# Empty rows of blocks are not gathered, places are permuted evenly, and the last 12 blocks add into sums in SBUF

## The chip, the cores and the metric

The kernel runs on one core of a Trainium2 chip. The metric is the device time of one execution in microseconds. TensorE (PE) multiplies, VectorE (DVE), ScalarE (ACT) and GpSimd (POOL) do the elementwise work, and 16 DMA engines, shared by all queues, move data between DRAM and SBUF. Two queues matter here: the one that SyncE (SP) feeds carries the weights, and the one that POOL feeds carries the gathers and scatters of rows.

## The reference, cut to what matters

One post-norm layer on x (512 tokens of 1024): a mixer of sparse and differential attention, attention into 256 memory tokens, then a mixture of experts; each is followed by a LayerNorm of `ALPHA * h + sublayer(h)`. The change concerns the experts alone:

```
scores = sigmoid(xf @ router_w)                      # 512 x 64
top_e  = top_k(scores + router_bias, 8)              # 8 experts of 64 for a token
gates  = scores[top_e] / sum(scores[top_e]) * 2.5
for e in experts:
    rows = tokens that chose e
    acc[rows] += swiglu(xf[rows], w_gate[e], w_up[e], w_down[e]) * gates
h = layer_norm(ALPHA * xf + acc + shared_swiglu(xf))
```

Each expert has 3.146 MB of fp32 weights (gate and up 1024 x 256 each, down 256 x 1024). 512 tokens of 8 experts make 4096 rows in all.

## The kernel before, in words

The attention parts run first (to about 580 us). Then the router ranks the experts by their number of rows, and they are done in 66 blocks: four fixed experts, 60 by rank, and two blocks with the overflow of the two largest. A rank has a fixed capacity from the list `CAPS` (128 down to 48 places; two of 160), 5392 places in all, so 1296 are empty. Counted from the reference's own inputs, the empty places are 296 in the first four blocks, 379 in blocks 4 to 23, 417 in blocks 24 to 53 (179 of them in 40 to 53) and 204 in the last twelve blocks, which have 656 places.

`meta` lists the rows of up to four ranks at a time: `one_hot` compares the places with each token's position, four small matmuls turn that into numbers, and `finish_meta` makes from them a gather index (`gidx`: an empty place reads row 0), a scatter index (`sidx`: an empty place goes to a spare row behind the 512 real ones) and the gate (`gsl`). `gather` (L1220) fetches the rows of a block by an indirect DMA into a tile `xg` (three buffers), `AHEAD` = 2 blocks ahead. A block of more than 64 rows is wide: its weights are split into two parts (`split_w`) and multiplied in three matmuls. From about block 38 on blocks are narrow (`narrow_block`): TensorE transposes `xg` into `xn` (L1268, L1271), multiplies with gate and up in plain fp32 (L1280), ACT makes `sg` (L1299), DVE `hm` (L1304), which is transposed into `ht` (L1313, L1315) and multiplied with `wd` (L1291) one block later, and ACT copies the output into `y` (L1294).

`scatter` (L1332) adds `y` to the rows of `acc`, a tensor in DRAM that holds the residual and the shared expert, by an indirect DMA with accumulation. All scatters write the same tensor, so each waits until the one before has landed. POOL issues gathers and scatters in the order of its program. SP issues the weight loads (L1226, L1235), `LEAD` = 9 loads of 1 MB ahead of the block that uses them, when one of the 18 free buffers of the pool `slots` is there; weights, their split parts and `y` (one buffer for two blocks) share that pool. After the last scatter (L1332, last of 66) `acc` is read back into `h` by four loads (L1625), and the last LayerNorm (L171, L1639) writes the output.

Of the kernel before, what the change touches and what calls it, by code (L numbers as in the profile page):

```python
# [19 lines left out]
P = 128  # L20
# [20 lines left out]
BIG_AT = (30, 50)  # L41
# [5 lines left out]
CAPS = ([128] * FIX + [160, 160, 128, 128] + [112] * 4 + [96] * 14 + [80] * 12 + [64] * 19 + [48] * 7)  # L47
HALF = 64
# [10 lines left out]
def encoder_layer(  # L59
# [927 lines left out]
    slot_id = cst.tile([P, P + 32], F32, name="slot_id")  # L987
# [4 lines left out]
    def dispatch_consts():  # L992
        jp = wk([P, P], name="jp")
        nc.gpsimd.iota(jp, pattern=[[1, P]], base=0, channel_multiplier=-1, allow_small_or_imprecise_dtypes=True)
        nc.vector.tensor_scalar(tri, jp, 0.0, None, op0=OP.is_gt)
        nc.vector.memset(ones, 1.0)
        nc.gpsimd.iota(slot_id, pattern=[[1, P + 32]], base=0, channel_multiplier=0,
                       allow_small_or_imprecise_dtypes=True)
# [42 lines left out]

    posf = cst.tile([P, NT, FIX], F32, name="posf")
# [132 lines left out]
    gidx = cst.tile([P, NEXP + 2], I32, name="gidx")  # L1175
# [12 lines left out]
    def one_hot(poscol, first=0, w=P):  # L1188
        oh = wk([P, NT, P], F32R, name="oh")[:, :, 0:w]
        nc.vector.tensor_tensor(oh, slot_id[:, None, first:first + w].to_broadcast([P, NT, w]),  # L1190
                                poscol.to_broadcast([P, NT, w]), op=OP.is_equal)
        return oh
# [7 lines left out]
    def meta(cols):  # L1200
# [4 lines left out]
        po, va = (posf, valf) if cols[-1][1] < FIX else (pos, vals)  # L1205
        for e, (c, r, first) in enumerate(cols):
            ohs.append(one_hot(po[:, :, r:r + 1], first, w))
# [6 lines left out]
        finish_meta(ps[0:w, 0:n * 4].rearrange("p (e v) -> p e v", v=4), n, gidx[0:w, s], sidx[0:w, s], gsl[0:w, s], w)  # L1214
# [68 lines left out]
    def narrow_out(m, ht, wd, n):  # L1283

        if m % 2 == 0:
            Y["y"] = slot([P, 2, D], name="y")
        y = Y["y"][:, m % 2, :]
        ps = bank()
        for j in range(2):
            for c in range(2):  # L1290
                nc.tensor.matmul(ps[HALF * c:HALF * c + n, :], lhsT=ht[:, j, 0:n], rhs=wd[:, j, c * 512:(c + 1) * 512],  # L1291
                                 start=j == 0, stop=j == 1)
        for c in range(2):
            nc.scalar.copy(y[0:n, c * 512:(c + 1) * 512], ps[HALF * c:HALF * c + n, :])  # L1294
        return y

# [93 lines left out]
    metas = [[(r, r, 0) for r in range(a, min(a + GRP, NEXP))] for a in range(FIX + 2, NEXP, GRP)]  # L1390
# [4 lines left out]
    NB = len(blocks)  # L1395
    W, XG, GS = {}, {}, {}
# [18 lines left out]
    def fetch_x(m):  # L1415
        if m < NB:
            _, _, n, c = blocks[m]
            XG[m] = gather(gidx[:, c:c + 1], n)
# [62 lines left out]
    def finish(m, ht, n, wd, si):  # L1481
        if narrow(m):
            y = narrow_out(m, ht, wd, n)
# [3 lines left out]
        scatter(y, si, n)  # L1487
# [6 lines left out]
    def narrow_block(m, X, xt, gs, si):  # L1494
        r, _, n, _ = blocks[m]
        step = 3 * step_of[r]
        ps = bank()
        w = W[r]
        narrow_mm(xt, w, n, ps, range(KH))
        yield 0.45 * KH, 0.0  # L1500
        ht = expert_h(*BEFORE[0][0:2])
        narrow_mm(xt, w, n, ps, range(KH, KD))
        yield 0.9, 0.0
# [8 lines left out]
        yield 0.8, 0.0  # L1512
# [3 lines left out]
    def experts():  # L1516
# [48 lines left out]
        finish(NB - 1, expert_h(*BEFORE[0][0:2]), *BEFORE[0][1:])  # L1565

# [23 lines left out]
    with tc.For_i(0, left, 1) as k:  # L1590
# [15 lines left out]
        gi = small.tile([P, 1], I32, name="gi", bufs=2)  # L1606
        si = small.tile([P, 1], I32, name="si", bufs=2)
        gs = small.tile([P, 1], F32, name="gs", bufs=2)
        finish_meta(ps[:, 0:4].rearrange("p (e v) -> p e v", v=4), 1, gi, si, gs)
        xg = gather(gi)  # L1610
# [5 lines left out]
        ht = expert_h(expert_mid(expert_gate(pg), pu, gs))  # L1616
        for c in range(2):
            y = expert_out(0, ht, w3[2], c)
        scatter(y, si)
# [3 lines left out]
    h3 = [slot([P, 2, D], name="h") for _ in range(2)]  # L1623
    for t in range(NT):
        nc.sync.dma_start(h3[t // 2][:, t % 2, :], acc[t * P:(t + 1) * P, :])  # L1625
    st = []
    for t in range(NT):
        h = h3[t // 2][:, t % 2, :]
# [5 lines left out]
    for t in range(NT):  # L1634
        h = h3[t // 2][:, t % 2, :]
# [38 lines left out]
```

## Time and profile before

| | us |
|---|---|
| median of 3 runs | 1315.51 |
| lowest, highest | 1314.42, 1317.23 |
| profiled execution, its own time | 1310.08 |
| its span in the trace | 1308.3 |
| TensorE busy in the span | 1155.8 (88%) |
| VectorE, ScalarE, GpSimd busy | 748.5, 562.0, 439.5 |

The busy times are averages over stages with different limits: from 640 to 850 us the wide blocks, from 850 to 1187 us wide and then narrow ones, from 1187 to 1271 us the last blocks up to the last matmul, and after that the last scatters and the LayerNorm. The rows by stage are shown below. The profiled execution is 5.4 us under the median of the three timed runs.

### The profile page before, as it was taken

What the parts mean: (1) busy time and instruction counts of PE and PEld (TensorE: products, weight loads), DVE (VectorE), ACT (ScalarE), POOL (GpSimd) and SP (SyncE); (2) the same over time, 40 slices, a digit from 0 to 9 for tenths busy, and PEclk for the clock granted to TensorE, in tenths of its full rate; (3) what the DMA queues carried; (4) which work ended last, traced back from release to release, by engine and by line L of the source; (5) the groups of instructions that cost most, each with busy time, mean ns of one, the idle gap of its engine ahead of it and who ended that gap; (6) DMA issues with size and microseconds to landing.
All of it is one profiled execution on the core that took longest, in us unless ns stands there. A gap on an engine that the chain in (4) does not pass through costs nothing. (4 is left out here: it accounts for less than half of the span.)

```text
span 1308.3 us, 20859 instructions
## 1 busy us (share of the span) xinstructions
PE 1155.8 (88%) x7768; PEld 908.2 (69%) x7768; DVE 748.5 (57%) x1617; ACT 562.0 (43%) x1006; POOL 439.5 (34%) x288
## 2 busy tenths in 40 slices
PE   3999999999898899889999999999899988897770
PEld 2887778988898898878778777777667544553330
DVE  7168986566865557787767777666465211311114
ACT  3235456644454453335555556555454211321122
POOL 4333444542236343552212323232213222223213
PEclk9999999998999899999999999999999989998995
DMA  7322234463326256688999999999999999999974
GB/s 225 86 74 65 58 103 114 121 202 116 126 67 210 63 185 208 226 332 329 299 289 331 352 347 362 332 359 359 350 367 338 350 347 387 363 363 353 349 279 141
DMA packets 136807, 324.67 MB, mean 248 GB/s; under 512 B 12001, under 2 KB 94945, under 8 KB 111873
## 3 DMA queue, kind: packets, MB, share of 16 engines
q1 hardware_dynamic: 119984, 275.83, 58.2%
q0 software_dynamic: 13632, 46.80, 14.8%
q8 instruction: 62, 1.02, 0.3%
q10 hardware_dynamic: 3088, 0.69, 0.2%
q14 instruction: 41, 0.33, 0.1%
HBM read 288.10 MB, written 35.19 MB: 247 GB/s over the span
## 5 line engine op out<-in xcount | busy, mean ns | idle before, releaser
L95 POOL TENSOR_TENSOR whl<-wraw,whl 128x1024 fp32r<-128x1024 f32 x81 | 195.9, 2419 | 265.4 <-ACT whl L94 239.4
L1244 DVE TENSOR_TENSOR whl<-wraw,whl 128x1024 fp32r<-128x1024 f32 x152 | 182.9, 1231 | 85.7 <-ACT whl L1243 79.6
L1332 POOL DMA_INDIRECT acc<-y,sidx x66 | 104.8, 1587 | 361.5 <-DMA acc<-y,sidx 161.4
L101 PE MATMUL ps<-whl,xt 128*96 128x256 f32 (+4 forms) x640 | 184.3, 288 | 5.6 <-ACT whl L1243 3.9
L103 PE MATMUL ps<-whl,xt 128*96 128x256 f32 (+4 forms) x640 | 179.8, 281 | 1.9 <-DVE xt L95 1.9
L102 PE MATMUL ps<-whl,xt 128*96 128x256 f32 (+4 forms) x640 | 179.6, 281 | 0.6 <-DVE whl L1244 0.6
L1243 ACT CAST whl<-wraw 128x1024 fp32r<-128x1024 f32 x152 | 152.5, 1053 | 27.9 <-DMA wraw<-in_e_w_gate_dram 20.0
L1327 PE MATMUL ps<-wd,ht 128*96 128x512 f32 (+4 forms) x320 | 147.1, 603 | 4.0 <-DVE ht L1315 3.8
L1280 PE MATMUL ps<-wraw,xn 128*64 128x256 f32 (+1 forms) x832 | 116.8, 404 | 27.0 <-DMA wraw<-in_e_w_up_dram 12.2
L1220 POOL DMA_INDIRECT xg<-rows,gidx x66 | 76.5, 1159 | 160.3 <-PE ps L1252 62.5
L1299 ACT ACTIVATE sg<-ps 64x256 f32<-64x256 f32 (+6 forms) x66 | 25.0, 378 | 239.6 <-PE ps L1280 127.1
L94 ACT CAST whl<-wraw 128x1024 fp32r<-128x1024 f32 x91 | 95.4, 1048 | 57.1 <-PE ps L103 46.5
L101 PEld LDWEIGHTS ps<-whl,xt 128*96 128x96 f32 (+4 forms) x640 | 104.3, 163 | 6.8 <-ACT whl L1243 4.1
L103 PEld LDWEIGHTS ps<-whl,xt 128*96 128x96 f32 (+4 forms) x640 | 104.3, 163 | 2.9 <-DVE xt L95 2.6
L1280 PEld LDWEIGHTS ps<-wraw,xn 128*64 128x64 f32 (+1 forms) x832 | 60.6, 140 | 65.0 <-DMA wraw<-in_e_w_up_dram 15.8
L102 PEld LDWEIGHTS ps<-whl,xt 128*96 128x96 f32 (+4 forms) x640 | 104.5, 163 | 1.1 <-DVE whl L1244 0.7
L1327 PEld LDWEIGHTS ps<-wd,ht 128*96 128x96 f32 (+4 forms) x320 | 49.5, 164 | 72.9 <-issue 66.0
L1315 DVE COPY ht<-ps 128x128 f32<-128x128 f32 (+6 forms) x66 | 21.4, 324 | 96.3 <-PE ps L1313 96.3
L1328 ACT COPY y<-ps 96x512 f32<-96x512 f32 (+4 forms) x80 | 46.3, 582 | 68.8 <-PE ps L1327 67.4
L1304 DVE SCALAR_TENSOR_TENSOR hm<-ps,og,sg 64x256 f32<-64x256 f32 (+4 forms) x54 | 36.8, 681 | 58.0 <-ACT sg L1299 48.8
L101 PE MATMUL ps<-xTh,whl 128*128 128x512 f32 (+1 forms) x168 | 65.6, 390 | 0.0
L103 PE MATMUL ps<-xTh,whl 128*128 128x512 f32 (+1 forms) x168 | 63.8, 380 | 0.0
(421 smaller groups left out, 2756.7 us busy)
## 6 DMA issues: line engine op xcount, KB each, us to landing
wraw<-in_e_w_gate_dram SPq DMA_DIRECT2D x64, 1024.0 KB, 18.8
wraw<-in_e_w_up_dram SPq DMA_DIRECT2D x64, 1024.0 KB, 15.7
wd<-in_e_w_down_dram SPq DMA_DIRECT2D x64, 1024.0 KB, 18.0
wraw<-in_w_in_dram SPq DMA_DIRECT2D x21, 512.0 KB, 3.7
wraw<-in_m_wkv_dram SPq DMA_DIRECT2D x16, 512.0 KB, 4.2
wraw<-in_m_wq_dram SPq DMA_DIRECT2D x16, 512.0 KB, 3.9
wraw<-in_m_wo_dram SPq DMA_DIRECT2D x16, 512.0 KB, 3.9
wraw<-in_w_o_dram SPq DMA_DIRECT2D x12, 512.0 KB, 3.5
```

Of the source, the lines that this page charges most:

```text
L94: nc.scalar.copy(hi, src)
L95: eng.tensor_sub(lo, src, hi.bitcast(F32))
L101: nc.tensor.matmul(ps, lhsT=a, rhs=b, start=start, stop=False)
L102: nc.tensor.matmul(ps, lhsT=a, rhs=bl, start=False, stop=False)
L103: nc.tensor.matmul(ps, lhsT=al, rhs=b, start=False, stop=stop)
L1220: nc.gpsimd.indirect_dma_start(out=xg[0:n, :], out_offset=None, in_=rows, in_offset=bass.IndirectOffsetOnAxis(ap=gi[0:n, :], axis=0))
L1243: nc.scalar.copy(hi[v], w[i][v])
L1244: lo_eng.tensor_sub(lo[v], w[i][v], hi[v].bitcast(F32))
L1280: nc.tensor.matmul(ps[HALF * i:HALF * i + n, 0:256], lhsT=xt[:, k, 0:n], rhs=w[i][:, k, :], start=k == 0, stop=k == KD - 1)
L1327: nc.tensor.matmul(ps[0:n, :], lhsT=ht[:, j, 0:n], rhs=wd[:, j, cs], start=j == 0, stop=j == 1)
L1328: nc.scalar.copy(y[0:n, cs], ps[0:n, :])
L1332: nc.gpsimd.indirect_dma_start(out=acc, out_offset=bass.IndirectOffsetOnAxis(ap=si[0:n, :], axis=0), in_=y[0:n, :], in_offset=None, comput ...
```

## The change

1. `gather` takes `sidx`, with a bound of the last real row: an index beyond it, that of an empty place, is skipped and moves nothing. `gidx` goes. The scatters of the empty places into spare rows stay.
2. Places are numbered by tables (`place_of`, small POOL iotas) that spread a rank's real rows evenly over the block's partitions. `meta` therefore groups only ranks of equal capacity; the second of the two experts of 160 is done at block 48 and not at 50.
3. The last `SUMMED` = 12 blocks (54 to 65, all narrow) have no scatter. `summed_out` writes the output of a block as a pair of fp32r parts `yp`, two blocks of 64 partitions in one tile, and for each pair of blocks `add_sums` multiplies it with a one-hot matrix of the tokens: 8 steps of two 128 x 512 matmuls and a DVE add into `sums`, two tiles of `slots` with the whole `acc`. `start_sums` takes five buffers at block 55, `load_sums` loads `acc` into `sums` on POOL's queue at block 56, after the scatter of block 53. Steps are interleaved with the blocks (`flush`), four in a block; twelve stand behind the last block. The LayerNorm reads `sums`; the four loads of `h` go. The lead of the weights is 10 loads in the last blocks.

```
-    def finish_meta(pv, n, gi, si, gs, w=P):
-        nc.vector.tensor_copy(gi, pv[:, :, 0])
+    def finish_meta(pv, n, si, gs, w=P):
...
+    def place_of(n, first):
...
+                        nc.gpsimd.iota(v, pattern=[[1, b], [16, hi - lo]], base=first + g * b + 16 * ((lo - g) % m),
+                                       channel_multiplier=0, allow_small_or_imprecise_dtypes=True)
...
     def gather(gi, n=P):
         nc.gpsimd.indirect_dma_start(out=xg[0:n, :], out_offset=None, in_=rows,
-                                     in_offset=bass.IndirectOffsetOnAxis(ap=gi[0:n, :], axis=0))
+                                     in_offset=bass.IndirectOffsetOnAxis(ap=gi[0:n, :], axis=0),
+                                     bounds_check=SEQ - 1, oob_is_err=False)
...
+    def load_sums():
+        for u in range(2):
+            a = slot([P, 2, D], name="sums")
+            for t in range(2):
+                nc.gpsimd.dma_start(a[:, t, :], acc[(2 * u + t) * P:(2 * u + t + 1) * P, :])
+                ACC.append(a[:, t, :])
...
+    def add_sums(oh, yp):
+        for t in range(NT):
+            for c in range(2):
+                cs = slice(c * 512, (c + 1) * 512)
+                ps = bank()
+                for l in range(2):
+                    nc.tensor.matmul(ps, lhsT=oh[:, t * P:(t + 1) * P], rhs=yp[:, l, cs], start=l == 0, stop=l == 1)
+                nc.vector.tensor_add(ACC[t][:, cs], ACC[t][:, cs], ps)
+                yield
...
+    def summed_out(m, ht, wd, n, si):
...
+        for cs, v in halves:
+            nc.scalar.copy(yp[r, 0, cs], v)
+        for cs, v in halves:
+            nc.vector.tensor_sub(yp[r, 1, cs], v, yp[r, 0, cs].bitcast(F32))
+        if i % 2:
+            oh = OHS[1][p % 3]
+            one_hot_rows(oh, STF.pop(p))
+            READY.append(add_sums(oh, PAIR.pop(p)))
...
     def finish(m, ht, n, wd, si):
-        if narrow(m):
-            y = narrow_out(m, ht, wd, n)
+        if m >= M0:
+            summed_out(m, ht, wd, n, si)
+        elif narrow(m):
+            scatter(narrow_out(m, ht, wd, n), si, n)
...
+        if m == M0 + 1:
+            start_sums()
+        if m == M0 + 2:
+            load_sums()
...
         finish(NB - 1, expert_h(*BEFORE[0][0:2]), *BEFORE[0][1:])
+        FL.extend(READY)
+        flush(16)
...
-    h3 = [slot([P, 2, D], name="h") for _ in range(2)]
-    for t in range(NT):
-        nc.sync.dma_start(h3[t // 2][:, t % 2, :], acc[t * P:(t + 1) * P, :])
```

POOL's program around the end of the scatters, of before; `xg` are gathered rows, the line with `acc` is a scatter, and the second row is the scatter of block 53:

```order
L1220 DMA xg<-rows,gidx 64x1024
L1332 DMA acc<-y,sidx 640x1024
L1220 DMA xg<-rows,gidx 48x1024
L1332 DMA acc<-y,sidx 640x1024
L1220 DMA xg<-rows,gidx 48x1024
L1332 DMA acc<-y,sidx 640x1024
L1220 DMA xg<-rows,gidx 48x1024 x2
L1332 DMA acc<-y,sidx 640x1024 x2
```

The same place after; L1327 are the four loads of `sums`, and the scatter ahead of them is that of block 53:

```order
L1245 DMA xg<-rows,sidx 64x1024
L1430 DMA acc<-y,sidx 640x1024
L1320 IOTA tk 128x512
L1245 DMA xg<-rows,sidx 64x1024
L1430 DMA acc<-y,sidx 640x1024
L1245 DMA xg<-rows,sidx 48x1024 x2
L1327 DMA sums<-acc 128x1024 x4
L1245 DMA xg<-rows,sidx 48x1024 x2
```

The loads stand behind the gathers of blocks 59 and 60, ahead of those of blocks 61 and 62, and no scatter follows.

DVE's program from the `hm` of block 57 to that of block 58, of before (numbers are those of the tiles):

```order
L1304 SCALAR_TENSOR_TENSOR hm_12665<-ps_12615,og_12432,sg_12654 64x128x2
L1406 COPY og_12980<-gsl_138 48x1
L1408 COPY og_12980<-order_132 1x1
L1271 COPY xn_12667<-ps_12674 128x256
L1315 COPY ht_12700<-ps_12697 128x2x64
L1304 SCALAR_TENSOR_TENSOR hm_12733<-ps_12684,og_12500,sg_12723 64x128x2
```

After, from the first add into `sums`, the first such row behind the `hm` of block 57, on (the two tiles of `sums` hold tokens 0 to 255 and 256 to 511; the `xn` of 48 is that of block 59):

```order
L1341 TENSOR_TENSOR sums_12731<-sums_12731,ps_12828 128x512
L1341 TENSOR_TENSOR sums_12731<-sums_12731,ps_12832 128x512
L1297 COPY xn_12859<-ps_12866 128x256
L1341 TENSOR_TENSOR sums_12731<-sums_12731,ps_12872 128x512
L1341 TENSOR_TENSOR sums_12731<-sums_12731,ps_12876 128x512
L1413 COPY ht_12915<-ps_12912 128x2x64
L1341 TENSOR_TENSOR sums_12734<-sums_12734,ps_12917 128x512
L1381 TENSOR_TENSOR yp_12653<-ps_12847,yp_12653 64x512 x2
L1341 TENSOR_TENSOR sums_12734<-sums_12734,ps_12921 128x512
L1402 SCALAR_TENSOR_TENSOR hm_12946<-ps_12899,og_12635,sg_12933 64x128x2
L1297 COPY xn_12948<-ps_12955 128x4x48
L1341 TENSOR_TENSOR sums_12734<-sums_12734,ps_12961 128x512
```

Between the two `hm`, which had an `xn` and an `ht` between them, there now stand the first six adds into `sums`; those of tokens 0 to 127 come ahead of the `xn` of block 58, those of 256 to 383 ahead of its `hm`, those of the last 128 behind the `xn` of block 59.

DVE's program at its end, after (before, the `ht` of the last block is the end, ahead of the LayerNorm):

```order
L1413 COPY ht<-ps 128x2x48
L1341 TENSOR_TENSOR sums<-sums,ps 128x512
L1381 TENSOR_TENSOR yp<-ps,yp 48x512 x2
L1341 TENSOR_TENSOR sums<-sums,ps 128x512 x11
```

Eleven of the last twelve adds stand behind the last part of `yp`.

## Rows read from the trace of the kernel before

**Rows 1.** The page: span, and the busy share of the DMA engines by slice.

```profile
span 1308.3 us, 20859 instructions
...
DMA  7322234463326256688999999999999999999974
```

**Rows 2.** Windows: stretch, its length, busy of PE, PEld, DVE, ACT, POOL, clock, DMA.

```profile
640.00:850.00 210.00, 206.48 (x1417) 163.48 (x1416) 152.06 (x282) 117.40 (x174) 56.15 (x37) 1.00 1.00 332
850.00:1187.00 337.00, 304.69 (x2109) 199.20 (x2109) 136.14 (x310) 121.16 (x208) 89.88 (x66) 0.96 1.02 358
1187.00:1271.00 84.00, 66.08 (x417) 30.47 (x412) 11.57 (x28) 16.44 (x37) 18.96 (x16) 0.90 0.97 341
1173.76:1181.55 7.79, 6.52 (x52) 3.50 (x51) 1.59 (x5) 2.76 (x6) 2.28 (x2) 1.00 1.03 345
1271.00:1290.00 19.00, 0.00 (x0) 0.00 (x0) 0.08 (x1) 0.37 (x1) 4.06 (x3) 0.61 0.36 78
```

**Rows 3.** DMA queues from 577 to 586 us: packets, MB, share of 16 engines.

```profile
q0 software_dynamic: 288, 1.05, 37.1%
```

**Rows 4.** DMA queues from 1000 to 1250 us: q1 weights, q0 gathers and scatters.

```profile
q1 hardware_dynamic: 10513, 76.55, 79.9%
q0 software_dynamic: 4064, 13.31, 22.0%
```

**Rows 5.** DMA queue from 1286 to 1295 us, the loads of `h`.

```profile
q1 hardware_dynamic: 576, 2.10, 64.3%
```

**Rows 6.** Timeline of ACT: outputs of blocks 40 and 53 (start, duration).

```profile
1044.23 1.17 ACT L1294 COPY y<-ps 64x512 f32<-64x512 f32 x2
...
1166.41 1.17 ACT L1294 COPY y<-ps 64x512 f32<-64x512 f32 x2 [1.31 <-PE ps L1291]
```

**Rows 7.** Timeline of POOL: scatters of blocks 40, 53 and 54.

```profile
1050.66 1.43 POOL L1332 DMA_INDIRECT acc<-y,sidx  x1 [5.34 <-DMA acc<-y,sidx]
...
1185.57 1.42 POOL L1332 DMA_INDIRECT acc<-y,sidx  x1 [5.33 <-DMA acc<-y,sidx]
...
1194.11 1.44 POOL L1332 DMA_INDIRECT acc<-y,sidx  x1 [5.89 <-DMA acc<-y,sidx]
```

**Rows 8.** Timeline of DVE: the `hm` of block 57.

```profile
1187.06 0.67 DVE L1304 SCALAR_TENSOR_TENSOR hm<-ps,og,sg 64x256 f32<-64x256 f32 x1 [1.17 <-ACT sg L1299]
```

**Rows 9.** Timeline of PE, early: two fp32r matmuls of 128 x 512.

```profile
62.54 0.40 PE L102 MATMUL ps<-xTl,whl 128*128 128x512 f32 x1
62.77 0.39 PE L103 MATMUL ps<-xTh,whl 128*128 128x512 f32 x1
```

**Rows 10.** Timeline of the end, all engines.

```profile
1266.84 0.66 DVE L1304 SCALAR_TENSOR_TENSOR hm<-ps,og,sg 48x256 f32<-48x256 f32 x1 [5.88 <-ACT sg L1299]
...
1268.23 1.92 PE L1291 MATMUL ps<-wd,ht 128*48 128x512 f32 x8 [0.35 <-DVE ht L1315]
...
1270.20 1.17 ACT L1294 COPY y<-ps 48x512 f32<-48x512 f32 x2 [3.39 <-PE ps L1291]
...
1277.04 1.35 POOL L1332 DMA_INDIRECT acc<-y,sidx  x1 [3.46 <-DMA acc<-y,sidx]
1281.80 1.35 POOL L1332 DMA_INDIRECT acc<-y,sidx  x1 [3.41 <-DMA acc<-y,sidx]
1286.57 1.76 SPq L1625 DMA_DIRECT2D h<-acc  x4
1289.92 1.28 DVE L171 BATCH_NORM_STATS2 st<-h 128x6 f32<-128x512 f32 x2 [21.74 <-DMA h<-acc]
```

**Rows 11.** Groups of L95 on DVE by form: count, busy, mean ns, idle before.

```profile
L95 DVE TENSOR_TENSOR pt<-ps,pt 128x512 fp32r<-128x512 f32 x20 | 13.6, 683 | 4.6 <-ACT pt L94 4.5
```

**Rows 12.** Timeline of POOL at the program's start.

```profile
9.89 0.14 POOL L1130 IOTA lim<- 128x4 f32 x1
12.61 1.73 POOL L186 TENSOR_TENSOR x<-x,gb 128x512 f32<-128x512 f32 x1 [2.57 <-DMA gb<-in_ln_in_b_dram]
```

More of the change, by code (lines that the diff above doesn't have):

```diff
@@ L1205, in meta @@
         po, va = (posf, valf) if cols[-1][1] < FIX else (pos, vals)
+        assert all(min(CAPS[r] - first, P) == w for _, r, first in cols)
+        tab = place_of(w, cols[0][2])
         for e, (c, r, first) in enumerate(cols):
-            ohs.append(one_hot(po[:, :, r:r + 1], first, w))
+            ohs.append(one_hot(po[:, :, r:r + 1], first, w, tab))
             if e:
@@ L1292, in narrow_out @@
                                  start=j == 0, stop=j == 1)
+        return ps
+    def narrow_out(m, ht, wd, n):
+        if m % 2 == 0 or "y" not in Y:
+            Y["y"] = slot([P, 2, D], name="y")
+        y = Y["y"][:, m % 2, :]
+        ps = narrow_down(ht, wd, n)
         for c in range(2):
@@ L1295, in narrow_out, with flush @@
         return y
+    def summed_out(m, ht, wd, n, si):
+        i = m - M0
+        p, base = i // 2, HALF * (i % 2)
+        if i % 2 == 0:
+            PAIR[p] = YP[p % 3]
+            STF[p] = small.tile([P, 1], F32, name="stf", bufs=3)
+            if min(blocks[m][2], blocks[m + 1][2]) < HALF:
+                nc.vector.memset(STF[p], -1.0)
+        yp, stf = PAIR[p], STF[p]
+        r = slice(base, base + n)
+        if n < HALF:
+            nc.gpsimd.memset(yp[base + 32:base + HALF].bitcast(F32), 0.0)
+        ps = narrow_down(ht, wd, n)
+        nc.scalar.copy(stf[r], si[0:n])
+        halves = [(slice(c * 512, (c + 1) * 512), ps[HALF * c:HALF * c + n, :]) for c in range(2)]
+        for cs, v in halves:
[6 more added lines that the diff above has]
+            READY.append(add_sums(oh, PAIR.pop(p)))
+    def flush(n):
+        while n and FL:
+            if next(FL[0], 0) == 0:
+                FL.pop(0)
+            else:
+                n -= 1
     def expert_gate(pg, n=P):
@@ L1389, in encoder_layer @@
     step_of = {r: n for n, r in enumerate(seq)}
-    metas = [[(r, r, 0) for r in range(a, min(a + GRP, NEXP))] for a in range(FIX + 2, NEXP, GRP)]
+    metas = []
+    for r in range(FIX + 2, NEXP):
+        if not metas or len(metas[-1]) == GRP or CAPS[metas[-1][0][0]] != CAPS[r]:
+            metas.append([])
+        metas[-1].append((r, r, 0))
     metas.append([(FIX, FIX, 0), (FIX + 1, FIX + 1, 0)])
@@ L1395, in encoder_layer @@
     NB = len(blocks)
+    M0 = NB - SUMMED
+    assert all(blocks[m][2] <= HALF and not blocks[m][1] for m in range(M0, NB)) and (NB - M0) % 2 == 0
     W, XG, GS = {}, {}, {}
@@ L1417, in fetch_x @@
             _, _, n, c = blocks[m]
[L1418 removed]
+            XG[m] = gather(sidx[:, c:c + 1], n)
     def routing():
@@ L1465, in top_up @@
         ahead = 16 + used // 2 if "listed" in done else 0
-        while fetched[0] < min(max(used + LEAD, ahead), 3 * NEXP):
+        lead = LEAD + (1 if used > 3 * step_of[blocks[M0][0]] else 0)
+        while fetched[0] < min(max(used + lead, ahead), 3 * NEXP):
             next(g_w)
@@ L1486, in finish @@
                 y = expert_out(m, ht, wd, c, n)
-        scatter(y, si, n)
+            scatter(y, si, n)
     def rows_x(m):
@@ L1616, in encoder_layer @@
         ht = expert_h(expert_mid(expert_gate(pg), pu, gs))
+        stf = small.tile([P, 1], F32, name="stf", bufs=3)
+        nc.vector.tensor_copy(stf, si)
+        oh, yp = OHS[1][0], YP[0]
+        one_hot_rows(oh, stf)
         for c in range(2):
-            y = expert_out(0, ht, w3[2], c)
-        scatter(y, si)
+            cs = slice(c * 512, (c + 1) * 512)
+            ps = bank()
+            for j in range(2):
+                nc.tensor.matmul(ps, lhsT=ht[:, j, :], rhs=w3[2][:, j, cs], start=j == 0, stop=j == 1)
+            split(yp[:, 0, cs], yp[:, 1, cs], ps)
+        for _ in add_sums(oh, yp):
+            pass
     gb = G3[0]
-    h3 = [slot([P, 2, D], name="h") for _ in range(2)]
-    for t in range(NT):
-        nc.sync.dma_start(h3[t // 2][:, t % 2, :], acc[t * P:(t + 1) * P, :])
     st = []
     for t in range(NT):
-        h = h3[t // 2][:, t % 2, :]
+        h = ACC[t]
         if t % 2:
```

63 lines of the change are left out of this document (46 added, 17 removed).

## The prediction

> **What bounds the kernel now.** I read the page first: in its slices by fortieths the DMA engines are at nine tenths from about 690 us on [rows 1]. Whether that binds is read from windows, stage by stage. From 640 to 850 us TensorE is busy 206.5 of 210 us at full clock: wide blocks, bound by TensorE although the DMA engines are full as well. From 850 to 1187 us it idles 337.0 - 304.7 = 32.3 us and the DMA share is 1.02, so transfers bind. In the last blocks it is busy 66 of 84 us at a mean granted clock of 0.90, and one narrow block holds 6.52 us of matmuls [rows 2]. From 1271 to 1290 us TensorE does nothing. The timeline of the end says why: the last matmul ends at 1270.15, three scatters follow, each 4.77 us after the one before, then `acc` is read back, and the LayerNorm starts at 1289.92 [rows 10]. So there are three places to cost: the transfer-bound stage (A), the last twelve blocks (B) and the tail (C).
>
> **Prices of a row.** The quiet window of two gathers of 128 rows has 256 rows (1.05 MB of 4 KB) in 37.1% of 9 us of 16 engines: 0.209 us of one engine for a gathered row, 13 ns of all [rows 3]. From 1000 to 1250 us gathers and scatters moved 13.31 MB, 3250 rows, in 22.0% of 250 us: 0.271 us a row. With about as many scattered as gathered, a scattered row costs 0.333 us, 21 ns of all engines. The weights moved 76.55 MB in 79.9%, so 2.6 us for a MB; the 3.146 MB of an expert are 8.2 us [rows 4]. Reading 2.1 MB of `acc` took 64.3% of 9 us, 5.8 us [rows 5].
>
> **A, rows not gathered before the last twelve blocks.** 417 empty places in blocks 24 to 53 fall into the transfer-bound stage: 417 x 13 ns = 5.4 us of all engines, and as TensorE waits there, of time. The 379 in blocks 4 to 23 (4.9 us) lie under a TensorE that is 98% busy, the 296 of the first four before that stage, and I count them as nothing. I take **-5.4**. Bounds: 0 (a skipped index may still cost a descriptor, and no row of before shows one) and -10.3 (the wide stage's rows help as well, through weights that run further ahead). The tables of places are POOL iotas; one of before takes 0.14 us. Sixteen of them stand at the program's start, 2.2 us in a place where POOL waits 2.57 us for a load [rows 12], so they are hidden; without that gap they would cost their 2.2 us once. Seven later tables are regenerated between scatters, where POOL has 5 us of idle time [rows 7]; a one-hot of DVE waits for each, but lists rows that come blocks later. The dropped copy of the gather index is one small DVE operation for a group, on an engine that idles there: nothing.
>
> **B, up to the last matmul.** Before, from the end of block 57's middle step (`hm`, 1187.06, [rows 8]) to the last matmul's end at 1270.15 [rows 10] are 83.1 us: eight blocks of 9.9 us, and 4 us behind the last `hm`. A block then needs 8.2 us of weights, and no scatter; its gather is 37 real rows, 0.5 us: 8.7 us by transfers. TensorE has 6.52 us and four steps of two fp32r matmuls of 128 x 512, which start 0.23 us apart early in the program [rows 9]: 8.4 us. Undisturbed, that is 8 x 8.7 + 4 = 73.6, a gain of 9.5.
>
> But the load of `sums` disturbs it. Its four loads stand on POOL behind the scatter of block 53 and read what that writes. Before, that scatter starts at 1185.57 and has landed when the next starts at 1194.11 [rows 7], 7.0 us behind the `hm` of block 57. DVE's first add stands right behind that `hm`; behind the add stand the `xn` of block 58, its `ht`, its `hm`: TensorE runs dry at once. The third of the four loads must land before the `hm` of block 58 can follow (two adds, 2.1 us with the `hm` itself); then come seven blocks of 8.6 us (weights have run ahead, so at TensorE's pace or a little more) and the 4 us. The last matmul then ends at T + 66.3 us, T being the landing of the third load after the `hm` of block 57. T = 16.8 changes nothing, T under 7.3 gives the whole 9.5.
>
> When do the loads start? The output of block 40 is done at 1045.4, that of 53 at 1167.6 [rows 6]; their scatters start at 1050.66 and 1185.57 [rows 7]. So the chain of scatters takes 10.4 us a block where the blocks take 9.4, and its lag grows from 5 to 18 us. In the quiet tail one cycle is 4.77 us with three rows an engine [rows 10]; under load it is 5.6 us more with four scattered and four gathered rows, five more: 1.1 us a row. Of the gathers of blocks 40 to 53, 179 rows go, 0.8 an engine and block: 0.9 us of a cycle, 11 us over thirteen, less the 2 that the blocks themselves gain. The chain may thus land 9 us earlier, 2 us ahead of that `hm`, or not at all earlier, 7.0 behind it. I take the middle, 2.5.
>
> How long do they take? 32 rows an engine: 5.8 us alone [rows 5]. Above it the bound is all that can be open when DVE stops, because weights wait for buffers then: ten loads ahead less the three of the block in work, 7 x 2.7 + 5.8 = 25 us. At the loaded 1.1 us a row 32 rows would need 35, more than that bound, so I go near the upper end and take 21 for all four, 15.8 for three. T = 18.3, and B = 18.3 + 66.3 - 83.1 = **+1.5**.
>
> The Trainium skill, "DMA: Bandwidth & Descriptors", section "Queues, rings and completion order", says that a DMA engine alternates between its queues by packets of some 9 to 17 descriptors. By that rule 32 rows are two to four packets, each behind one packet of weights; with 0.34 us for a descriptor of 8 KB (2.7 us of a MB over eight) I get an estimate of 18 to 19 us for the four loads, and the sum would be about 2 us lower. No row of before shows two long transfers of both queues side by side, so the sum keeps my 21.
>
> Pool buffers: `sums`, the one-hots and `yp` take seven of 18, which leaves eleven for loads, and the lead is ten; two `y` buffers end. I cost that at nothing; if one load fewer fits, it shows as a wait of SP for a buffer in the last blocks.
>
> **C, the tail.** Before: 1270.15 to 1289.92, 19.8 us. After: two casts on ACT, 1.17 us for the like-sized copies [rows 10], one exposed DVE part and eleven adds from PSUM at 0.68 us each [rows 11] (the 24 matmuls, 5.5 us, lie beside them), and an estimate of 1 us to pass the overflow loop: 1.2 + 0.7 + 7.5 + 1.0 = 10.4. **-9.4**, with bounds -8 and -10.5. What follows is the LayerNorm, unchanged, read from `sums`.
>
> **The sum.** -5.4 + 1.5 - 9.4 = -13.3 us on the profiled 1310.1: 1296.8. The profiled execution is 5.4 us under the median of the timed runs; on that median it is 1302.
>
> **Rivals.** *The sums are there in time.* The chain lands early by the full 9 us and the loads take the quiet rate nearly (three within 9 us): T under 7.3, B = -9.5, the sum -24.3, 1291. The lag's growth by a mere 1 us a block speaks for it, as less than that must go; the DMA share of 0.97 in that stage [rows 2] speaks against the quiet rate. Chance 0.25. *Skipping saves nothing,* neither engine time nor time in the chain: A = 0, T = 7.0 + 15.8 = 22.8, B = +6.0, sum -3.4, 1312. For it: rows of the scatters for empty places stay, and no row prices a skipped one. Chance 0.15. *Slower: the load of the sums starves TensorE.* It starts 7.0 behind the `hm` and pays 1.1 us a row because weights keep coming: T = 7.0 + 24 x 1.1 = 33.4, B = +16.6. In the stage of before the clock of 0.90 lost 8.4 us in 84 beside 18 us of idle TensorE [rows 2], half a microsecond for each idle one; a stop of some 25 us may lose 4 more. Sum -5.4 + 20.6 - 9.4 = +5.8, 1321. It decides from T of about 34 without the clock, 30 with it. Against it is the bound by open loads. Chance 0.10. My forecast, T between 8 and 23 with skipped rows saving something: 0.50, from 1293 to 1311.
>
> **Range and chances.** 1287 (the first rival with A near its bound) to 1318, between the second and the third, which leaves less than 2 in 10 outside. A difference of 0.2%, 2.6 us, is about what a measurement of this kernel can tell from no change. Faster holds the forecast, the first rival and most of the second: 0.83. Same, 0.07, takes the edge between the second and the third; slower, 0.10, is the third.
>
> **What the changed profile would show.** For A: fewer rows on the gather queue, and TensorE idle some 5 us less between 850 and the block that was at 1187 us. For B: where the scatter of block 53 lands beside the `hm` of block 57, and the idle time of DVE before the first adds into `sums`, ended by the DMA of `sums`: some 15 us in all by my sum, none by the first rival, 25 or more by the third. Then blocks 8.6 us apart. For C: eleven adds back to back behind the last matmul and 10 us to the LayerNorm. I am wrong if DVE doesn't wait for `sums`, if blocks 59 to 65 stay 10 us apart, or if the stage before 1187 us is no shorter.

## The result and the profile after

The changed kernel takes 1312.0 us (median of 15 runs, 1301.0 to 1317.3) against 1317.2 for the kernel before on the same chip (15 runs); the ratio is 0.9945, with a 95% interval of 0.9929 to 0.9961. It is faster, by 7 us by this ratio and 5 by the medians, where 13 were forecast. Gains in us below are those of the ratios. The profiled execution of after took 1313.5 us, a little over its median; that of before (1310.1) was 7 us under it, so that the two traces side by side show no gain at all. They have to be read by stage.

The page of after: span, TensorE's row, DMA engines by slice.

```profile
span 1311.6 us, 21278 instructions
PE 1177.6 (90%) x7864; PEld 925.3 (71%) x7864; DVE 798.7 (61%) x1685; ACT 565.2 (43%) x1018; POOL 447.0 (34%) x335
...
DMA  7222133464416255788999999999999999999941
```

In the last two slices the DMA engines are now busy for 4 and 1 tenths; before, it was 7 and 4 [rows 1]. The windows of after, with the columns of [rows 2]; the first two lie ahead of the experts, where nothing was changed but POOL's tables.

```profile
100.00:200.00 100.00, 95.67 (x412) 73.30 (x410) 85.31 (x220) 48.01 (x97) 39.05 (x21) 0.95 0.25 70
300.00:400.00 100.00, 94.48 (x670) 88.31 (x670) 70.61 (x181) 51.98 (x113) 29.61 (x14) 0.95 0.35 107
640.00:850.00 210.00, 207.55 (x1423) 164.70 (x1422) 150.75 (x268) 121.46 (x179) 63.15 (x51) 1.00 0.98 332
850.00:1191.70 341.70, 304.89 (x2134) 201.59 (x2132) 141.62 (x317) 122.58 (x215) 91.47 (x71) 0.96 1.01 354
1191.70:1215.30 23.60, 18.46 (x88) 9.20 (x90) 7.89 (x19) 4.43 (x13) 5.16 (x7) 0.78 1.02 384
1215.30:1281.00 65.70, 63.26 (x406) 31.31 (x401) 42.52 (x72) 12.60 (x27) 14.81 (x10) 1.00 0.69 265
```

From 100 to 200 us the granted clock was 1.00 in the profile before and 0.95 here, from 300 to 400 us 0.97 and 0.95. The first `hm` of the experts comes 6.4 us later (613.5, before 607.1). I take this for the clock of one execution: in the profiles of the seventeen kernels below, whose program is the same up to there but for the gather, it comes between 606.9 and 618.3. The rest is told from the `hm` of block 0 on. Up to block 57 after is 1.8 us quicker (578.2, before 580.0). From the `hm` of block 57 (1191.7) to the last matmul of the last block (1281.0) it takes 89.3 us, before 83.1 [rows 8, 10]. From there to the first of the LayerNorm on VectorE it takes 11.7 us, before 19.8 [rows 10].

What stands between blocks 56 and 59 is a chain of waits. POOL's timeline of after, from the scatter of block 52 on:

```profile
1178.02 1.43 POOL L1430 DMA_INDIRECT acc<-y,sidx  x1 [7.46 <-DMA acc<-y,sidx]
1178.97 1.08 POOL L1320 IOTA tk<- 128x512 f32 x1
...
1186.67 1.43 POOL L1430 DMA_INDIRECT acc<-y,sidx  x1 [5.29 <-ACT yp L1379]
...
1194.96 2.23 POOL L1327 DMA_DIRECT2D sums<-acc  x4 [4.32 <-DMA acc<-y,sidx]
```

VectorE's timeline of after beside it:

```profile
1180.08 0.43 DVE L1321 CAST tokens<-tk 128x512 fp32r<-128x512 f32 x1 [9.23 <-POOL tk L1320]
1180.42 0.28 DVE L1413 COPY ht<-ps 128x128 f32<-128x128 f32 x1
...
1191.72 0.66 DVE L1402 SCALAR_TENSOR_TENSOR hm<-ps,og,sg 64x256 f32<-64x256 f32 x1
...
1192.55 1.25 DVE L1331 TENSOR_SCALAR ohs<-tokens,stf 128x512 fp32r<-128x512 f32 x3
...
1203.93 1.29 DVE L1341 TENSOR_TENSOR sums<-sums,ps 128x512 f32<-128x512 f32 x2 [10.01 <-DMA sums<-acc]
...
1207.71 1.28 DVE L1341 TENSOR_TENSOR sums<-sums,ps 128x512 f32<-128x512 f32 x2 [2.16 <-DMA sums<-acc]
...
1212.58 0.69 DVE L1341 TENSOR_TENSOR sums<-sums,ps 128x512 f32<-128x512 f32 x1 [3.38 <-PE ps L1348]
...
1215.32 0.68 DVE L1402 SCALAR_TENSOR_TENSOR hm<-ps,og,sg 64x256 f32<-64x256 f32 x1
...
1216.86 0.69 DVE L1341 TENSOR_TENSOR sums<-sums,ps 128x512 f32<-128x512 f32 x1 [0.48 <-DMA sums<-acc]
```

And TensorE's:

```profile
1180.76 3.68 PE L1348 MATMUL ps<-wd,ht 128*64 128x512 f32 x8 [5.20 <-DVE ht L1413]
...
1193.16 2.04 PE L1340 MATMUL ps<-yp,ohs 128*128 128x512 f32 x4 [3.50 <-DVE ohs L1331]
1195.13 3.68 PE L1348 MATMUL ps<-wd,ht 128*64 128x512 f32 x8
...
1205.61 1.93 PE L1306 MATMUL ps<-wraw,xn 128*64 128x256 f32 x8 [3.11 <-DVE xn L1297]
```

The load of the sums is where it was looked for: it starts 3.2 us behind the `hm` of block 57, VectorE waits 10 us for the first tile, and the last tile is there 21.9 us after the first load was issued. (By the packet rule of the Trainium skill, "DMA: Bandwidth & Descriptors", section "Queues, rings and completion order", the estimate was 18 to 19; the trace is nearer to the 21 I had taken.) The first add on the third tile starts at 1212.58, 20.9 us behind that `hm`. The row names TensorE, but the matmuls of that add were done by 1209.6; what came last is the landing of the tile. But two waits stand ahead of it that I had not named. VectorE's cast of the token numbers waits 9.2 us for an iota that stands on POOL behind the scatter of block 52, with the `ht` and `hm` of block 56 behind it; and TensorE's first matmuls for the sums wait 3.5 us for the one-hots. Behind the waits of 5.2 and 3.5 us the same eight matmuls with `wd` take 3.68 us; at 1210.46 they take 1.89. From 1180.8 to 1184.3 us the granted clock is 0.50, the lower of the two levels, and from 1210.5 to 1212.3 it is 1.00. Then 65.7 us follow in which TensorE is busy for 63.3 at full clock, with a DMA share of 0.69. The end of after, VectorE and the last block's last matmuls:

```profile
1274.14 0.68 DVE L1402 SCALAR_TENSOR_TENSOR hm<-ps,og,sg 48x256 f32<-48x256 f32 x1 [0.61 <-ACT sg L1397]
...
1276.11 0.69 DVE L1341 TENSOR_TENSOR sums<-sums,ps 128x512 f32<-128x512 f32 x1 [1.29 <-PE ps L1340]
1276.79 1.39 DVE L1381 TENSOR_TENSOR yp<-ps,yp 48x512 fp32r<-48x512 f32 x2
1278.21 0.69 DVE L1341 TENSOR_TENSOR sums<-sums,ps 128x512 f32<-128x512 f32 x1
1278.81 0.25 DVE L1413 COPY ht<-ps 128x96 f32<-128x96 f32 x1
...
1279.12 1.92 PE L1348 MATMUL ps<-wd,ht 128*48 128x512 f32 x8 [2.32 <-DVE ht L1413]
...
1283.90 6.67 DVE L1341 TENSOR_TENSOR sums<-sums,ps 128x512 f32<-128x512 f32 x11
1292.77 1.29 DVE L172 BATCH_NORM_STATS2 st<-sums 128x6 f32<-128x512 f32 x2 [2.20 <-ACT sq L264]
```

The last `ht` comes 4.7 us behind the last `hm`, behind two adds and two subtractions; before it was a copy right behind its transposes, so the last matmul ends 6.9 us after that `hm`, not 3.3 [rows 10]. Eleven adds stand back to back, as forecast.

### The profile page after: what moved, and what is told of

Its sections match the earlier page's. It is cut to its first block, busy times and chain, and to the rows that moved or that the text cites. A ratio compares the mean times of both kernels' runs of the same rounds, so it can differ in the third digit from the quotient of the medians.

```text
span 1311.6 us, 21278 instructions
## 1 busy us (share of the span) xinstructions
PE 1177.6 (90%) x7864; PEld 925.3 (71%) x7864; DVE 798.7 (61%) x1685; ACT 565.2 (43%) x1018; POOL 447.0 (34%) x335
## 3 DMA queue, kind: packets, MB, share of 16 engines
q0 software_dynamic: 13360, 40.91, 12.9%
## 5 line engine op out<-in xcount | busy, mean ns | idle before, releaser
L1430 POOL DMA_INDIRECT acc<-y,sidx x54 | 88.1, 1631 | 324.2 <-DMA acc<-y,sidx 186.6
L1245 POOL DMA_INDIRECT xg<-rows,sidx x66 | 78.2, 1185 | 131.6 <-PE ps L1294 50.6
L1306 PE MATMUL ps<-wraw,xn 128*64 128x256 f32 (+1 forms) x832 | 109.1, 394 | 13.8 <-ACT xn L1299 5.7
L95 ACT CAST whl<-wraw 128x1024 fp32r<-128x1024 f32 x91 | 95.4, 1049 | 60.0 <-PE ps L104 46.7
L1306 PEld LDWEIGHTS ps<-wraw,xn 128*64 128x64 f32 (+1 forms) x832 | 56.8, 136 | 49.8 <-ACT xn L1299 10.0
L102 PE MATMUL ps<-xTh,whl 128*128 128x512 f32 (+1 forms) x168 | 67.3, 400 | 0.0
L103 PE MATMUL ps<-xTl,whl 128*128 128x512 f32 (+1 forms) x168 | 65.3, 389 | 0.0
L104 PE MATMUL ps<-xTh,whl 128*128 128x512 f32 (+1 forms) x168 | 65.3, 389 | 0.0
L1348 PE MATMUL ps<-wd,ht 128*64 128x512 f32 (+1 forms) x208 | 55.0, 632 | 8.7 <-DVE ht L1413 8.7
```

What stands on the lines that cost most here:

```text
L95: nc.scalar.copy(hi, src)
L102: nc.tensor.matmul(ps, lhsT=a, rhs=b, start=start, stop=False)
L103: nc.tensor.matmul(ps, lhsT=a, rhs=bl, start=False, stop=False)
L104: nc.tensor.matmul(ps, lhsT=al, rhs=b, start=False, stop=stop)
L1306: nc.tensor.matmul(ps[HALF * i:HALF * i + n, 0:256], lhsT=xt[:, k, 0:n], rhs=w[i][:, k, :], start=k == 0, stop=k == KD - 1)
L1430: nc.gpsimd.indirect_dma_start(out=acc, out_offset=bass.IndirectOffsetOnAxis(ap=si[0:n, :], axis=0), in_=y[0:n, :], in_offset=None, comput ...
```

## The experiments

Ratios are to the kernel before, timed beside it on the same chip; the runs come from several chips, so two kernels are compared by their ratios. One profile of such a kernel scatters by some 5 us, so times of stages are read from several profiles together where there are several.

**Rows kept** (x1_rows_kept). An empty place reads row 0 again, by a gather index of its own as before:

```
-            XG[m] = gather(sidx[:, c:c + 1], n)
+            XG[m] = gather(gidx[:, c:c + 1], n)
```

> The changed kernel, but an empty place gathers row 0 again (an index of its own for the gathers, as before); places and sums stay. Theory 1 (a skipped row saves next to nothing, because its place in the queue still has to be served): ratio to the kernel before 0.993 to 0.997, like the changed kernel's 0.9945. Rival (skipping saves my 5.4 us in the transfer-bound stage): about 5 us more than the changed kernel, ratio 0.998 to 0.999.

1317.6 us, ratio 0.9981 (0.9959 to 1.0004). Skipping is worth 0.36% in the changed kernel, 4.7 us with an interval of 1 to 8: the rival's number, and theory 1 is unlikely.

**No sums** (x3_no_sums). The kernel before with places and skipping alone (`place_of`, `metas` and `gather` of after; scatters, `h` and the end of before).

> The kernel before with the even places and the skipped rows alone; all blocks scatter, the end is as before. Theory 1: within 0.2% of the kernel before, ratio 0.998 to 1.002, with scatters as far apart as before. Rival (my term A): 5 us faster, 0.996. A second rival, that the tables of places cost time in the first 600 us: slower by up to 6 us, 1.003 to 1.005, and the first block as late as in the changed kernel's trace.

1306.2 us, 0.9899 (0.9862 to 0.9936): 13 us faster than before, and by the ratios faster than the changed kernel. All three expectations had too small a gain; theory 1 falls.

**Sums from zero** (x4_zero_sums).

```
-                nc.gpsimd.dma_start(a[:, t, :], acc[(2 * u + t) * P:(2 * u + t + 1) * P, :])
+            nc.gpsimd.memset(a, 0.0)
```

> The changed kernel, but the sums start from zero by two memsets on POOL and are never loaded, so the result lacks what stands in DRAM (the residual, the shared expert and the blocks 0 to 53). Theory 2 (the load of the sums stops VectorE and with it TensorE before block 58): no gap of 24 us between the middle steps of blocks 57 and 58, some 9 us instead, and 8 to 14 us less than the changed kernel: ratio 0.984 to 0.988. Rival (TensorE is the bound of the last blocks anyway, the stop is caught up later): at most 3 us less, 0.992 or above.

1310.5 us, 0.9948 (0.9923 to 0.9974), the changed kernel's ratio: theory 2 falls. The step from block 57 to 58 is still 16.8 us. Two reservations. The memset runs on POOL beside the one-hots of block 57, and these take 3.1 us here, 1.25 in the changed kernel: nearly 2 us of the step probably come from the edit. And in this kernel's profile and in those of the two other ones with zero sums below, 40.2 to 41.7 us pass from the last `hm` to the end of the span, where loaded sums with second parts have 37.4 to 38.5; some 3 us of it stand behind the last instruction on VectorE. I found no cause, and a gain of up to that much may hide there.

**Later steps** (x6_later_steps).

```
-        FL.extend(READY)
+        if m >= M0 + 5:
+            FL.extend(READY)
...
-        flush(2)
+        flush(3)
```

> The changed kernel with the steps of the sums kept back: they begin at block 59 and not at 57, three in each half of a block and not two, eight behind the last block and not twelve. Theory 2: the sums have landed when the first add is due, the stop goes, 7 to 11 us less than the changed kernel, ratio 0.986 to 0.989. Rival (the stop is only moved, or six steps a block lengthen the blocks by as much): ratio 0.993 to 0.996.

1316.8 us, 0.9986 (0.9964 to 1.0008). Neither holds: it is slower than the changed kernel. The stop at block 58 goes (10.7 us), but blocks 60 to 65 take 9.0 to 11.2 us each, and one 19.6.

**Token numbers from VectorE** (y1_tokens).

```
-        nc.gpsimd.iota(tk, pattern=[[1, SEQ]], base=0, channel_multiplier=0, allow_small_or_imprecise_dtypes=True)
-        nc.vector.tensor_copy(ohs[:, 0, :], tk)
+        for t in range(NT):
+            nc.vector.tensor_scalar(ohs[:, 0, t * P:(t + 1) * P], slot_id, float(t * P), None, op0=OP.add)
```

> The changed kernel, but the row of token numbers, which the one-hots are compared with, is made on VectorE from a table of the program's start (four adds of 128 x 128) and not by an iota on POOL, which stands there behind the scatter of block 52. Theory 3 (what is lost before block 58 is a chain of several waits; the first is VectorE's for that iota, 9.2 us, which holds back the ht and hm of block 56 and lets TensorE idle 5.2 us and fall to the lower clock): the step from block 55 to 56 is 7 to 8 us again and not 12.6, TensorE has no idle time of over 2 us before the last matmuls of block 55, and the kernel is 4 to 7 us faster than the changed one, ratio 0.989 to 0.992. Rival (the scatters' chain and the load of the sums set the end of the stop, so that a wait taken away before it makes the next one longer): within 2 us of the changed kernel, 0.993 to 0.996.

1311.4 us, 0.9941 (0.9919 to 0.9963). The wait of 5.2 us is gone from the trace, the time is not: the rival's number. Behind it TensorE now waits 2.9 us for weights of block 57, 3.5 for the one-hots, 2.3 for an `xn` behind the sums.

**Both** (y2_tokens_zero). The last two edits together.

> The kernel y1_tokens with sums that start at zero and are not loaded (the residual, the shared expert and blocks 0 to 53 are missing in the result). Theory 3: without the iota's wait the load of the sums becomes the last wait, so here its removal counts: 0.983 to 0.987, and no step of the blocks 55 to 65 above 12 us. Rival (TensorE's matmuls for the sums are the price, not any wait): 0.991 to 0.995, like x4_zero_sums.

1307.4 us, 0.9919 (0.9887 to 0.9950): 3 us under y1_tokens, within the intervals, and the longer tail of zero sums may hide as much again. The rival is nearer. A window of this kernel:

```profile
1206.00:1266.00 60.00, 60.00 (x400) 31.41 (x402) 41.27 (x66) 12.52 (x27) 16.66 (x11) 1.00 0.81 318
```

TensorE is busy for all of these 60 us. So what a wait costs ahead of them can't be caught up there, and transfers saved in them shorten nothing.

**Tokens and a later start** (y3_tokens_later). As y1_tokens, with `if m >= M0 + 4` ahead of `FL.extend(READY)`.

> The kernel y1_tokens with the first step of the sums at block 58 and not at 57, two in each half of a block as in the changed kernel, so that sixteen steps and not twelve stand behind the last block. Theory 3: the wait for the one-hots (3.5 us of TensorE) and most of the wait for the sums go, 8 to 12 us, and four more adds behind the last matmul cost 2.7: ratio 0.985 to 0.989. Rival (the stop moves along with the steps): 0.993 to 0.997.

1314.1 us, 0.9973 (0.9948 to 0.9999): the rival's number, but not its mechanism. No step behind block 57 is longer than 11.6 us in the trace. Without the stop the blocks are longer, and from the `hm` of block 57 to the last block's last matmul it takes 87.5 us, 87.9 in y1_tokens; four more steps stand behind.

**Places only** (y4_places_only). x3_no_sums with a gather index that reads row 0.

> The kernel x3_no_sums with a gather index of its own again, in which an empty place reads row 0: even places alone, nothing skipped, no sums. If skipping makes the 1.0% that x3_no_sums gained: 0.998 to 1.002. If the even places (real rows spread over all DMA engines) make it: 0.989 to 0.993. If each makes a part, as x1_rows_kept has it (skipping gave 3 to 5 us there): 0.993 to 0.997.

1318.7 us, 0.9997 (0.9971 to 1.0022). No gain by the places themselves can be told; skipping makes the 1.0%.

**Skipping in a part of the blocks** (z1_skip_early, and z2_skip_late with `m >= 24`).

```
+            skip = m < 24
+            XG[m] = gather((sidx if skip else gidx)[:, c:c + 1], n, skip)
```

> No sums, even places; empty places are skipped in blocks 0 to 23 alone (675 rows) and read row 0 in the later ones. My term A: these rows lie under a busy TensorE, so 0.998 to 1.002. Rival (theory 4: what the DMA engines save there is kept as weights that lie ready, and is paid out where TensorE waits for weights): 379 rows of blocks 4 to 23 at 13 ns are 4.9 us, 0.995 to 0.997.

1313.0 us, 0.9948 (0.9928 to 0.9969): 6.9 us for rows that I had counted as nothing. Its one trace doesn't show them behind the `hm` of block 0: from there to the end it takes 704.1 us, y4_places_only 703.8, z2_skip_late 694.9 and x3_no_sums 695.9.

> No sums, even places; empty places are skipped in blocks 24 to 65 alone (621 rows). My prices: 417 + 204 rows at 13 ns, 8.0 us, ratio 0.992 to 0.995. If theory 4 is right as well, this and z1_skip_early add up to the 1.0% of x3_no_sums. If rows pay by the queue and not by their bytes: at most 2 us, 0.998 to 1.000.

1310.9 us, 0.9929 (0.9906 to 0.9952): 9.4 us, where 8.0 were priced. The two add up to 1.2%, x3_no_sums gained 1.0%: they are the same within the intervals. Theory 4's size fits the timing; that weights lying ready carry it over is not shown.

**One matmul a step** (z3_one_part). y1_tokens without the second parts in the sums:

```
-                for l in range(2):
-                    nc.tensor.matmul(ps, lhsT=oh[:, t * P:(t + 1) * P], rhs=yp[:, l, cs], start=l == 0, stop=l == 1)
+                nc.tensor.matmul(ps, lhsT=oh[:, t * P:(t + 1) * P], rhs=yp[:, 0, cs], start=True, stop=True)
```

> The kernel y1_tokens with one matmul and not two for a step of the sums: the second parts of the outputs are left out of the sums (a loss of precision of the last 12 blocks' outputs). Theory 5 (from the stop on TensorE is the bound of the last blocks, 8.4 to 8.6 us each, with the transfers done some 20 us before it): four matmuls less a block, 0.9 us, 6 to 8 us for the stage: ratio 0.987 to 0.990. Rival (weights, or the load of the sums, set the pace): within 2 us of y1_tokens, 0.992 to 0.995.

1304.5 us, 0.9879 (0.9845 to 0.9912): theory 5's number. By the ratios 8 us go with half of the sums' matmuls, whose own time is a microsecond a block; the two ratios have intervals of 3 and 4 us to either side. The traces show a part of it: blocks 58 to 65 take 55.6 us, 58.8 in y1_tokens.

**No last scatters** (z4_no_last_scatters). x3_no_sums with `if m < NB - 12:` ahead of `scatter`.

> The kernel x3_no_sums in which the outputs of the last 12 blocks are computed and dropped (no scatter, no sums; they are missing in the result), and acc is read back at the end as before. It bounds what the sums could give at best. By my terms: the last blocks 8.7 us apart, 9 us less, and the three last scatters of 4.8 us gone, 14 us less: 0.972 to 0.976. If it is only 0.984 or above, the last scatters were not what the last blocks waited for.

1292.3 us, 0.9780 (0.9743 to 0.9817). The scatters of the last twelve blocks are worth 1.2%, 15.7 us, in a kernel that skips, within some 7 us. In its profile the last eight blocks take 8.6 us each, against 9.4 in x3_no_sums.

**What is left of the price.** Four kernels: u1_one_part_zero is z3_one_part with the memset of x4_zero_sums; u2_one_part doesn't make the second parts (the diff); u3_order is x3_no_sums with `BIG_AT = (30, 48)`; u4_one_part_later is u2_one_part with the start of y3_tokens_later.

```
-            nc.vector.tensor_sub(yp[r, 1, cs], v, yp[r, 0, cs].bitcast(F32))
...
-        YP.extend(slot([P, 2, D], F32R, name="yp") for _ in range(3))
+        for k in range(2):
+            both = slot([P, 2, D], F32R, name="yp")
+            YP.extend(both[:, l, :] for l in range(2 - k))
```

> The kernel z3_one_part (one matmul a step, second parts left out) with sums that start at zero and are not loaded, so the result also lacks the residual and all blocks up to 53. If the wait for the load is what is left of the sums' price: 8 to 12 us less than z3_one_part, 0.979 to 0.982, near z4_no_last_scatters. If TensorE and the start of the steps are: within 4 us, 0.985 to 0.988.

1305.9 us, 0.9906 (0.9877 to 0.9934): no gain over z3_one_part, so the load's wait is not what is left, unless the longer tail of zero sums (40.2 us, 38.3 there) hides it.

> The kernel z3_one_part in which the second parts are not made at all (two subtractions of VectorE a block go, two buffers hold the outputs and not three, so one more is there for weights); less precise outputs of the last 12 blocks, as there. If VectorE's order or buffers matter: 2 to 5 us less than z3_one_part, 0.984 to 0.987, and the tail 1.4 us shorter. If not: 0.987 to 0.989.

1299.9 us, 0.9843 (0.9813 to 0.9873), the fastest of the kernels with a whole result. The last `hm` stands 31.7 us ahead of the end, 37.4 in the changed kernel, and VectorE's timeline has the last `ht` 1.1 us behind it:

```profile
1268.03 0.66 DVE L1400 SCALAR_TENSOR_TENSOR hm<-ps,og,sg 48x256 f32<-48x256 f32 x1 [2.94 <-ACT sg L1395]
1269.10 0.26 DVE L1411 COPY ht<-ps 128x96 f32<-128x96 f32 x1 [0.41 <-PE ps L1409]
1271.81 7.26 DVE L1341 TENSOR_TENSOR sums<-sums,ps 128x512 f32<-128x512 f32 x12 [2.45 <-PE ps L1340]
```

> The kernel x3_no_sums with the second large expert at block 48 as in the changed kernel, and not at 50. No theory gives it a price: 0.988 to 0.992, like x3_no_sums. A rival, that the order and not the sums makes the difference between x3_no_sums and the changed kernel: 0.994 to 0.996.

1306.2 us, 0.9904 (0.9878 to 0.9929): the order of the large expert has no part that can be told.

> The kernel u2_one_part with the first step of the sums at block 58 and not 57 (16 steps behind the last block and not 12). With TensorE relieved a later start may hide the wait for the sums: 4 to 8 us less at the stop, 2.7 more in the tail: 0.982 to 0.986. If the stop only moves, as in y3_tokens_later: 0.988 to 0.992.

1306.2 us, 0.9918 (0.9892 to 0.9944): a later start loses again, 10 us against u2_one_part.

**The buffer** (u5_buffers). u2_one_part with three buffers for the outputs.

> The kernel u2_one_part with three buffers of the pool for the outputs, as in the changed kernel, and not two; one fewer for weights. If VectorE's subtractions, which stand ahead of the middle step and of the last blocks' ht, are the price: like u2_one_part, 0.982 to 0.987. If the buffer is: like z3_one_part, 0.986 to 0.990, with the last weights landing later.

1301.7 us, 0.9876 (0.9851 to 0.9900). The ratio lies in the range given for the buffer, near z3_one_part, but its interval overlaps u2_one_part's. The tail is as short as there (31.6 us) although the buffer is gone, so the tail is VectorE's. How much of the rest is the buffer stays open.

## Why the prediction was right in direction and too large

The gain came out at 7.2 us by the ratio, 5.2 by the medians, where 13.3 were forecast. The step that failed is B, "+1.5", with its rule "T = 16.8 changes nothing, T under 7.3 gives the whole 9.5": it lets the landing of the sums decide alone, from the `hm` of block 57 on. The other waits that the sums bring were put at nothing. The ratios of the kernels with even places show it:

| | without sums | with sums |
|---|---|---|
| empty rows gathered | 0.9997 (y4_places_only) | 0.9981 (x1_rows_kept) |
| empty rows skipped | 0.9899 (x3_no_sums), 0.9904 (u3_order) | 0.9945 (after) |

With the sums, skipping is worth 4.7 us, and A had 5.4. The sums, B and C together, were to bring 7.9 us; they bring 2 where rows are gathered and cost 5 to 6 where they are skipped. Each difference has an interval of 4 to 6 us to either side. By the stages of the two traces A is -1.8, B +6.2 and C -8.1, -3.7 in all.

**A, -5.4.** In its own stage A is near. Blocks 23 to 53 take 296.5 us on average in the eleven kernels with sums that skip in all blocks (294.7 to 298.7), and 300.2 in x1_rows_kept, which has the same order of blocks: some 4 us less, against a single trace. (The 1.8 us of the two traces stand in blocks 0 to 3, 34.6 us for 37.2 before; it is 33.8 to 34.1 in all the kernels above, also in those that skip nothing, so it is not skipping.) But little of it is left at block 57. Blocks 53 to 57 take 37.8 us in after, 30.5 before, and 33.8 in u3_order, which has the order of after and skips, without sums. The waits for the iota and for the `ht` and `hm` behind it stand there, and the prediction begins to count the sums at block 57. From 850 us to that `hm` TensorE idles 36.8 us, before 32.3, where 5 less were expected.

Another step of A is not borne out by the timing, and it made the gain too small, not too large: "the 379 in blocks 4 to 23 lie under a TensorE that is 98% busy, ... and I count them as nothing". Without sums, skipping in blocks 0 to 23 alone gave 6.9 us by its timing (z1_skip_early), and skipping everywhere 13 (x3_no_sums against y4_places_only). At 13 ns of all DMA engines the 1296 rows would be 16.8 us, and 13.0 without those of the first four blocks; the intervals don't tell these apart. The wide stage itself got no shorter: blocks 3 to 23 take 211.1 to 212.1 us in all the profiles with early skipping, 211.6 before. What is saved there would have to come out later. Blocks 23 to 30 take 72.3 to 75.1 us in the fourteen kernels that skip in all blocks and 76.8 to 77.0 in the three that skip nothing; further on the trace of z1_skip_early shows nothing of it. Where it comes out stays open. So it is in part luck that A is near in the changed kernel: by the timing rows that were left out pay as well, and with the sums less of what is saved reaches the end.

**B, +1.5.** The trace has +6.2: the `hm` of block 58 comes 23.6 us behind that of 57, where 20.4 were worked out; the seven blocks behind it take 8.4 us each and not 8.6; and the last matmul ends 6.9 us behind the last `hm` and not 4. The four loads took 21.9 us for the 21 worked out, and started at 3.2 for 2.5. That start is luck: it was to come from a quicker chain of scatters, which is not shown (see the last section). T is 20.9 and not 18.3, which gives 2.6 of the 4.7 us that B is off. But T does not decide alone. Without the load the step from block 57 to 58 is still 14.5 to 16.8 us (u1_one_part_zero, y2_tokens_zero, x4_zero_sums) and not 8.7: the one-hots and the lower clock behind TensorE's idle time stand there too. I had the one-hots and the token numbers in the diff and gave them no price. At the end 2.9 us more are lost, since the last `ht` queues behind two adds and two subtractions; I had 4 us there by the row of before. In u2_one_part, without the subtractions, the last matmul ends 3.3 us behind the last `hm`.

The blocks behind the stop were priced rightly, by "8.7 us by transfers. TensorE has ... 8.4 us". With transfers relieved TensorE is the bound without a gap (60.0 of 60 us in y2_tokens_zero), so nothing that is lost at the start is caught up. The prediction had that in its sum, but not that it makes A and B depend on each other.

**C, -9.4.** From the last matmul to the LayerNorm it is -8.1, inside the bounds: 10.4 were worked out, 11.7 are there. VectorE idles 2.2 us ahead of the LayerNorm, where 1 us was put down to pass the overflow loop.

**Together.** Leaving out the last scatters was worth 15.7 us (z4_no_last_scatters), and the sums cost 5 to 6 beside a kernel that skips, so the sums' own price is some 21 as an estimate, within some 5. By the timings half of their matmuls are 8 of it (the traces show 3 in seven blocks), and the second parts' subtractions and buffer up to 5 (u2_one_part). How the rest divides is not shown.

Of the rivals none came true by its condition: the sums were not there in time, skipping did save, and the kernel was not slower. But the numbers of the second one came: B = +6.0 and 1312 us, with +6.2 and 1312.0 measured. That is coincidence: it had the loads start 7.0 us behind the `hm` of block 57 and three of them take 15.8, and they started at 3.2 and took 17.7.

Skipping alone gives 1.0%, with the sums 0.36%. I take the reason to be that the end is then bound by TensorE, so that saved transfers buy little there: from the `hm` of block 58 to that of 65 TensorE is busy 61.2 of 62.4 us in x1_rows_kept and 58.7 of 58.8 in after, and the DMA share falls from 0.92 to 0.77. A version that by the ratios beats both kernels and computes the same is x3_no_sums, 0.9899; with outputs of the last blocks rounded to one fp32r part u2_one_part reaches 0.9843.

## What to carry to other kernels

When a change relieves one engine in a stage, work out the stage's floor for every engine anew, with all edits of the change in it: two prices as close as 8.7 and 8.4 us a block mean that the second is the bound as soon as the first falls, and that no wait ahead of it is caught up. Two savings that are priced on the same old stage do not add up if the first one changes what binds there: here skipping was worth 13 us alone and 4.7 with the sums. And an instruction that only prepares something (an iota, a one-hot) has a place in a queue: look what stands ahead of it there and who is behind the engine that waits for it. But to take one such wait away is worth nothing when the next one ends as late (y1_tokens).

## What the runs showed of the hardware

A skipped row of an indirect gather leaves a packet. The queues from 860 to 1180 us, packets, MB and share, of after with its count of packets:

```profile
DMA packets 18822, 113.22 MB, mean 354 GB/s; under 512 B 2955, under 2 KB 2955, under 8 KB 7082
...
q0 software_dynamic: 5616, 16.91, 22.6%
```

and of before:

```profile
DMA packets 18707, 114.31 MB, mean 357 GB/s; under 512 B 2460, under 2 KB 2460, under 8 KB 7081
...
q0 software_dynamic: 5628, 18.93, 24.2%
```

The two windows hold the same times, not quite the same blocks. The bytes fall by 2.0 MB (493 rows), the packets of the queue stay, and those under 512 B rise by 495. The queue's share falls by 1.6% of 320 us, 5.1 us of 16 engines, so that a skipped row saves 0.17 us of one engine, of the 0.21 that a gathered one takes [rows 3]. The chain of scatters, which I had expected up to 9 us earlier for it, is not clearly quicker: the scatter of block 53 starts 534 to 544 us behind the `hm` of block 3 in the fourteen profiles that skip in all blocks, 535 to 546 in the three that skip nothing. Beside the `hm` of block 57 it starts 5.1 us ahead in after, 1.5 before, and 12.9 in x1_rows_kept, which gathers every row.
